# The last part of an entry moved between the first two product groups of the chunk or down half behind it

## The chip, the cores and the metric

The kernel runs on one core of a Trainium2 chip. The core has several engines that run side by side, each with an instruction queue of its own: TensorE (PE; its weight loads are listed as PEld) does the matrix products, VectorE (DVE) and ScalarE (ACT) do elementwise work, GpSimd (POOL) does little here, and SyncE (SP) issues the loads. The metric is the device time of one execution in microseconds (us), as the median of several runs.

## The reference

The model is a decoder trunk of two layers on 512 tokens of width 1024. Each layer has a mixer between two half-step SwiGLU feed-forward networks (FFNs), so there are four FFNs, and they are what the change touches.

```python
def swiglu(h, w_gate, w_up, w_down):
    return (jax.nn.silu(h @ w_gate) * (h @ w_up)) @ w_down

for i in range(DEPTH):                 # DEPTH = 2, D_MODEL = 1024, D_FF = 2816
    x = x + 0.5 * swiglu(rmsnorm(x, ffn1_norm[i]), ...)
    x = x + mixer(rmsnorm(x, mix_norm[i]))       # gated linear attention, then stick-breaking
    x = x + 0.5 * swiglu(rmsnorm(x, ffn2_norm[i]), ...)
return rmsnorm(x, final_norm)
```

All of it is float32. The weights come from HBM once each.

## The kernel before

**Precision by three products.** A float32 operand is split into a high part `h` and the rest `l`. ScalarE writes `h` (a cast, L138) and VectorE subtracts it from the operand to get `l` (L139). A product is then three matmuls, high by high, low by high and high by low, into one PSUM bank.

**Seven products for eight.** Most gate and up projections are done in chunks of 256 columns by a scheme of Strassen's kind (`seven`, from L682): the chunk's weights and the normed input are cut into halves, and seven products of sums of these halves do the work of eight. The sums of the weights (`sums_12`, `sums_34`: L694, L695, L700, L701) are made by VectorE, and their high and low parts are split like any operand. A product here is one call of `prod` (the matmul is L709): four steps of three matmuls, twelve in all. A chunk is two entries. Body 1 makes the products w (with the first block of the weights), then q, then more into w, and then z; body 2 goes on with w, q and w. The accumulators live on: after the first product ScalarE copies w into a second bank, z (L736), and both are accumulated further. The fourth product goes into z and the third into w, and the next products read-modify-write those banks. In between, ScalarE or VectorE takes out what has become final: `gate` is the silu of a gate chunk (L719, ScalarE) or the multiplication by the gate in an up chunk (L722, VectorE), L755 is a VectorE sum that the second activation of a gate chunk waits for, and L806 and L807 split the hidden activations again.

**The down projection** has two forms. A plain entry (`down`) makes a few output blocks `ps_d`, each followed by an addition to the residual x on VectorE (L339). For two groups of the hidden columns a down half (`seven_down`) uses the seven-product scheme: its products are L384, its copies of w into z L402, and each of its results is added to x by VectorE (L390). Its body 1 makes w, q, t2 (into w) and z; body 2 makes t3 (into w), b22 (into q) and t4 (into w), with a copy of w into u3 (L429) behind t3.

**The queue of entries.** All the weight matrices are cut into entries, in one list `feed.q`. An entry's `body` is a generator that yields after each group of products. `Feed.start` takes the next entry. First it splits the weights of this entry and of up to two behind it, as far as four large units go; it also forms the sums of the entries ahead and issues the loads of up to six entries. Then it returns the body. `Feed.entries` (L183) runs entries one by one: start, then each group to its end. With `ordered` it puts each group's matmuls behind the last matmul issued so far (`tc.issue_after(st["pe"])`), so that TensorE keeps the order of the program. Beyond such ties a scheduler places the instructions of each engine, and each engine runs its own in order.

In each FFN the order from the third chunk on is, with G and U for a gate and an up chunk, d for a plain down entry and sd for a down half: d d G2 U2 G3 d U3 d G4 U4 sd G5 U5 G6 sd d U6 d G7 d U7 d G8 U8 sd G9 U9 sd d G10 U10, and then the plain entries at the end. The text calls the two halves behind U4 and G6 the first pair, and those behind U8 and U9 the second pair.

**Buffers.** The raw weights of a chunk lie in `raw` (two buffers), the split ones in `wh` and `wl` (four each), the sums in `s` (four), the chunk's outputs in tiles with the tag `t` (five); PSUM has eight banks that are given out in a fixed turn.

Of the kernel before, what the change touches and what calls it, by code (L numbers as in the profile page):

```python
# [10 lines left out]
F32 = mybir.dt.float32  # L11
# [7 lines left out]
P = 128  # L19
T = 512  # L20
# [26 lines left out]
def decoder(ctx: ExitStack, tc: tile.TileContext, a: dict, out: bass.AP):  # L47
# [43 lines left out]
    class Chunk:  # L91
        def __init__(self, src, n, m):
            self.src, self.n, self.m, self.t = src, n, m, None
            self.pool = None
            self.few = False
# [12 lines left out]
    class Entry:  # L108
# [3 lines left out]

        def __init__(self, units, body):
            self.units, self.body, self.W, self.views = units, body, None, None

        def view(self):

# [24 lines left out]
    class Feed:  # L142
        def __init__(self):
            self.q, self.pos, self.cur = [], 0, None

        def start(self):
            i = self.pos
# [35 lines left out]
        def entries(self, n, ordered=False):  # L183

            self.finish()
            for _ in range(n):
                body, more = self.start(), True
                while more:
                    with tc.issue_after(st["pe"]) if ordered else ExitStack():
                        more = next(body, self) is not self  # L190

    feed = Feed()

# [118 lines left out]
    def down(w, r0, nf, hs, part, nxt, late=0):  # L312


        nd = KD // nf
        src = w[r0 : r0 + nf * P, part * nd * P : (part + 1) * nd * P]
        ch = Chunk(src.rearrange("(f p) c -> p f c", p=P), nf, nd * P)
        ch.few = True

        def body(W):  # L320
            (wh, wl), = W
            acc = []

            def prod(m, fs):
                if m == len(acc):
                    acc.append(psum("ps_d"))
                s = slice(m * P, (m + 1) * P)
                for f in fs:
                    mm3(acc[m], wh[:, f, s], wl[:, f, s], hs[f][0], hs[f][1], f == 0, f == nf - 1)

            if late:
                for m in range(nd):
                    prod(m, range(nf - late))
            for m in range(nd):
                prod(m, range(nf - late if late else 0, nf))
                ps = acc[m]
                k = part * nd + m
                x = pair(xs[k])
                nc.vector.scalar_tensor_tensor(  # L339
                    out=x, in0=flat(ps), scalar=0.5, in1=x, op0=ALU.mult, op1=ALU.add  # L340
                )
                if nxt is not None:
                    nxt(k)
                yield

        feed.q.append(Entry([(ch, lambda t: t, nf, nd * P)], body))

    def seven_down(pool, w, r0, hs, part):

        H = T // 2
        lower, upper = (
            Chunk(w[r0 : r0 + 4 * P, c : c + 256].rearrange("(f p) c -> p f c", p=P), 4, 256)
            for c in (part * 256, 512 + part * 256)
        )
        lower.few = upper.few = True
        v = {}

        def halves():  # L360

            lo, up = (c.load().rearrange("p (c two) d -> p two c d", two=2) for c in (lower, upper))
            return lo[:, 0], lo[:, 1], up[:, 0], up[:, 1]

        def sums_12(_):
            a11, _, a21, a22 = halves()
            s = v["s12"] = pool().tile([P, 4, 256], F32, tag="s", bufs=4, name="s12")
            nc.vector.tensor_tensor(out=s[:, 0:2], in0=a21, in1=a22, op=ALU.add)
            nc.vector.tensor_tensor(out=s[:, 2:4], in0=s[:, 0:2], in1=a11, op=ALU.subtract)
            return s  # L370

        def sums_34(_):
            a11, a12, a21, _ = halves()
            s = pool().tile([P, 4, 256], F32, tag="s", bufs=4, name="s34")
            nc.vector.tensor_tensor(out=s[:, 0:2], in0=a11, in1=a21, op=ALU.subtract)
            nc.vector.tensor_tensor(out=s[:, 2:4], in0=a12, in1=v["s12"][:, 2:4], op=ALU.subtract)
            return s

        def prod(ps, w, k0, m, b, first):
            for c in range(2):  # L380
                bh, bl = (turns(t) for t in hs[c][b])
                wh, wl = (t[:, k0 + c, m * P : (m + 1) * P] for t in w)
                for n, (l_, r_) in enumerate(((wh, bh), (wl, bh), (wh, bl))):
                    st["pe"] = nc.tensor.matmul(  # L384
                        ps, l_, r_, start=first and c + n == 0, stop=c == 1 and n == 2, skip_group_check=True
                    ).ins

        def add(m, up, col, ps):
            x = pair(xs[part * 2 + m + 4 * up][:, col * H : col * H + H])
            nc.vector.scalar_tensor_tensor(out=x, in0=ps, scalar=0.5, in1=x, op0=ALU.mult, op1=ALU.add)  # L390

        def body_1(W):
            a11, s, v["a2"] = W
            ws, zs, qs = [], [], []
            for m in range(2):
                ws.append(psum("ps_w")[:, 0:H])
                prod(ws[m], a11, 0, m, "b11", True)
            for m in range(2):


                zs.append(psum("ps_z")[:, 0:H])
                nc.scalar.copy(zs[m], ws[m])  # L402
            yield

            ps = psum("ps_q")
            for m in range(2):
                qs.append(ps[:, m * H : (m + 1) * H])
                prod(qs[m], s, 0, m, "t1", m == 0)
            for m in range(2):
                add(m, 1, 1, flat(qs[m]))  # L410
            yield
            for m in range(2):
                prod(ws[m], s, 2, m, "t2", False)
                add(m, 0, 1, flat(ws[m]))
            yield
            for m in range(2):
                prod(zs[m], v["a2"], 0, m, "b21", False)
                add(m, 0, 0, flat(zs[m]))
            v["w"], v["q"] = ws, qs
            yield  # L420

        def body_2(W):
            (s,) = W
            ws, qs = v["w"], v["q"]

            u3 = pool().tile([P, 2, H], F32, tag="c", bufs=1, name="u3")
            for m in range(2):
                prod(ws[m], s, 0, m, "t3", False)
                nc.scalar.copy(pair(u3[:, m]), flat(ws[m]))  # L429
                add(m, 1, 1, pair(u3[:, m]))  # L430
            yield
            for m in range(2):
                prod(qs[m], s, 2, m, "b22", False)
            for m in range(2):
                add(m, 0, 1, flat(qs[m]))
            yield
            for m in range(2):
                prod(ws[m], v["a2"], 2, m, "t4", False)
                add(m, 1, 0, flat(ws[m]))
            yield  # L440

        units = [(lower, lambda t: halves()[0], 2, 256), (lower, sums_12, 4, 256), (lower, lambda t: halves()[1::2], 4, 256)]
        feed.q.append(Entry(units, body_1))
        feed.q.append(Entry([(lower, sums_34, 4, 256)], body_2))

    def back_tok(w, r0, nf, hs, done):
# [30 lines left out]
    st = {}  # L477
# [129 lines left out]
    class FFN:  # L607
# [76 lines left out]
        def seven(self, ch, group=None):  # L684
# [5 lines left out]
            s12, v = [None], {}  # L690
# [35 lines left out]
            def body_1(W):  # L726


                a11, s, a2 = W
                v["a2"] = a2  # L730
                v["w"], v["q"] = psum("ps_w"), psum("ps_q")
                z = psum("ps_z")[:, 0:H]
                w, q = (v[n][:, 0:H] for n in "wq")
                o0, o1 = v["o"] = [self.tp.tile([P, T], F32, tag="t", name=n) for n in ("o0", "o1")]
                prod(w, a11, 0, half(0, 0))
                nc.scalar.copy(z, w)  # L736
                yield
                prod(q, s, 0, lambda j: self.t_half(0, j))
                nc.scalar.copy(pair(o1[:, H:T]), flat(q))
                yield  # L740
                prod(w, s, 4, lambda j: self.t_half(1, j), first=False)
                nc.scalar.copy(pair(o0[:, H:T]), flat(w))
                yield
                prod(z, a2, 0, half(4, 0), first=False)
                gate(o0, 0, flat(z))
                yield

            def body_2(W):
                (s,) = W
                w, q = (v[n][:, 0:H] for n in "wq")  # L750
                o0, o1 = v["o"]
# [9 lines left out]
                if group is not None:  # L761
                    close_0(o0)
                gate(o1, H, pair(o1[:, H:T]))
                yield
                prod(w, v["a2"], 0, lambda j: self.t_half(3, j), first=False, c0=P)
                gate(o1, 0, flat(w))
                if group is not None:
# [18 lines left out]

            units = [(ch, lambda t: t[:, 0:4, 0:P], 4, P), (ch, sums_12, KD, P), (ch, lambda t: t[:, 4:8], 4, 256)]
            feed.q.append(Entry(units, body_1))
            feed.q.append(Entry([(ch, sums_34, KD, P)], body_2))

        def t_half(self, i, j):
# [1114 lines left out]
```

## Time and profile before

| | |
|---|---|
| median of three runs | 1781.2 us (1780.84 to 1781.41) |
| the profiled execution | 1780.26 us |
| its span in the profile | 1778.3 us |
| granted clock of TensorE | 1.000 |
| moved by DMA | 179.24 MB, mean 101 GB/s |

The span is the time from the first to the last instruction that the profile shows; the execution's own time is 2 us longer, for what lies around it. The median of the runs without a profile is 0.9 us above the profiled execution. In the rows, the first number of a timeline is the start in us from the beginning of the span, the second the duration; then come engine, line, operation, output and inputs by the program's names without buffer numbers, and in brackets how long the engine had been idle before, and which instruction ended that. Matmuls are pipelined: a new one starts before the last one has ended, so one reads their starts, not their durations.

### The profile page before, as it was taken

What the parts mean: (1) busy time and instruction counts of PE and PEld (TensorE: products, weight loads), DVE (VectorE), ACT (ScalarE), POOL (GpSimd) and SP (SyncE); (2) the same over time, 40 slices, a digit from 0 to 9 for tenths busy, and PEclk for the clock granted to TensorE, in tenths of its full rate; (3) what the DMA queues carried; (4) which work ended last, traced back from release to release, by engine and by line L of the source; (5) the groups of instructions that cost most, each with busy time, mean ns of one, the idle gap of its engine ahead of it and who ended that gap; (6) DMA issues with size and microseconds to landing.
All of it is one profiled execution on the core that took longest, in us unless ns stands there. A gap on an engine that the chain in (4) does not pass through costs nothing.

```text
span 1778.3 us, 31182 instructions
## 1 busy us (share of the span) xinstructions
PE 1760.1 (99%) x12714; PEld 1631.7 (92%) x12714; DVE 1538.5 (87%) x2527; ACT 1050.5 (59%) x1830; POOL 9.8 (1%) x24
## 2 busy tenths in 40 slices
PE   9999999999999999999999999999999999999998
PEld 8999999889888899999889999999888888999997
DVE  8999798786878999889798988977898679998986
ACT  7556455554655556555555555655888755565554
POOL 0000000100000000000000000000000000000000
PEclk9999999999999999999999999999999999999999
DMA  5433334322122333333333333322212233333331
GB/s 167 142 115 112 107 96 132 93 71 72 49 95 95 104 110 119 107 107 108 109 93 119 96 119 103 124 84 83 83 48 72 71 95 119 110 105 111 105 126 52
DMA packets 178755, 179.24 MB, mean 101 GB/s; under 512 B 4082, under 2 KB 170276, under 8 KB 178612
## 3 DMA queue, kind: packets, MB, share of 16 engines
q1 hardware_dynamic: 177760, 175.91, 31.6%
q8 instruction: 99, 1.62, 0.4%
q0 software_dynamic: 608, 1.05, 0.2%
q14 instruction: 44, 0.36, 0.1%
q10 hardware_dynamic: 244, 0.29, 0.0%
HBM read 175.17 MB, written 2.10 MB: 100 GB/s over the span
## 4 chain that ended last, share of the span: by engine, by line
PE 64%; DVE 25%; ACT 7%; issue 3%; DMA 1%; SPq 0%; DVEq 0%; ACTq 0%
PE ps_w L709 14%; PE ps_d L80 12%; PE ps_f L80 8%; DVE wl L139 7%; PE ps_q L709 7%; PE ps_t L80 5%; PE ps_z L709 3%; PE ps_b L80 3%; ACT wh L138 3%; PE ps_w L384 2%; DVE x L390 2%; DVE ts L816 1%; PE ps_q L384 1%; PE ps_z L1394 1%; DVE xn L800 1%
## 5 line engine op out<-in xcount | busy, mean ns | idle before, releaser
L139 DVE TENSOR_TENSOR wl<-raw,wh 128x1024 fp32r<-128x1024 f32 x241 | 254.9, 1058 | 58.1 <-ACT wh L138 57.5
L138 ACT CAST wh<-raw 128x1024 fp32r<-128x1024 f32 x241 | 221.6, 920 | 72.4 <-PE ps_f L80 21.5
L139 DVE TENSOR_TENSOR wl<-s,wh 128x1024 fp32r<-128x1024 f32 x176 | 214.2, 1217 | 42.2 <-ACT wh L138 41.9
L138 ACT CAST wh<-s 128x1024 fp32r<-128x1024 f32 x176 | 184.2, 1047 | 102.9 <-DVE s L701 25.7
L709 PE MATMUL ps_w<-th,wh 128*128 128x256 f32 x864 | 239.8, 278 | 3.7 <-ACT ps_z L736 2.7
L709 PE MATMUL ps_w<-th,wl 128*128 128x256 f32 x864 | 237.6, 275 | 0.0
L709 PE MATMUL ps_w<-tl,wh 128*128 128x256 f32 x864 | 237.6, 275 | 0.0
L709 PEld LDWEIGHTS ps_w<-th,wh 128*128 128x128 f32 x864 | 165.8, 192 | 7.4 <-ACT ps_z L736 7.1
L80 PE MATMUL ps_f<-xh,wh 128*128 128x512 f32 x432 | 166.8, 387 | 0.9 <-DVE x L260 0.9
L709 PEld LDWEIGHTS ps_w<-tl,wh 128*128 128x128 f32 x864 | 165.9, 192 | 0.0
L709 PEld LDWEIGHTS ps_w<-th,wl 128*128 128x128 f32 x864 | 165.8, 192 | 0.0
L80 PE MATMUL ps_f<-xh,wl 128*128 128x512 f32 x432 | 164.2, 380 | 0.5 <-DVE wl L139 0.5
L80 PE MATMUL ps_f<-xl,wh 128*128 128x512 f32 x432 | 164.0, 380 | 0.0
L80 PE MATMUL ps_d<-hl,wh 128*128 128x512 f32 x416 | 158.0, 380 | 0.9 <-DVE hl L807 0.8
L80 PE MATMUL ps_d<-hh,wh 128*128 128x512 f32 x416 | 157.7, 379 | 0.2 <-ACT hh L806 0.2
L80 PE MATMUL ps_d<-hh,wl 128*128 128x512 f32 x416 | 157.7, 379 | 0.0
L138 ACT CAST wh<-rawd 128x1024 fp32r<-128x1024 f32 (+1 forms) x100 | 82.9, 845 | 60.1 <-PE ps_d L80 45.2
L139 DVE TENSOR_TENSOR wl<-rawd,wh 128x1024 fp32r<-128x1024 f32 (+1 forms) x100 | 95.7, 961 | 14.7 <-ACT wh L138 14.7
L80 PEld LDWEIGHTS ps_f<-xh,wh 128*128 128x128 f32 x432 | 81.7, 189 | 12.1 <-DVE x L260 1.3
L80 PEld LDWEIGHTS ps_f<-xl,wh 128*128 128x128 f32 x432 | 81.7, 189 | 11.5
L80 PEld LDWEIGHTS ps_f<-xh,wl 128*128 128x128 f32 x432 | 81.7, 189 | 11.1 <-DVE wl L139 0.9
L339 DVE SCALAR_TENSOR_TENSOR x<-ps_d,x 128x512 f32<-128x512 f32 x120 | 79.8, 682 | 13.8 <-PE ps_d L80 13.7
(352 smaller groups left out, 5247.9 us busy)
## 6 DMA issues: line engine op xcount, KB each, us to landing
raw<-in_ffn_w_gate_dram SPq DMA_DIRECT2D x43, 1024.0 KB, 5.4
raw<-in_ffn_w_up_dram SPq DMA_DIRECT2D x43, 1024.0 KB, 5.3
rawd<-in_ffn_w_down_dram SPq DMA_DIRECT2D x84, 512.0 KB, 3.6
raw<-in_gla_w_in_dram SPq DMA_DIRECT2D x12, 1024.0 KB, 5.3
raw<-in_sb_w_in_dram SPq DMA_DIRECT2D x16, 512.0 KB, 3.7
raw<-in_gla_w_out_dram SPq DMA_DIRECT2D x4, 1024.0 KB, 5.2
raw<-in_sb_w_in_dram SPq DMA_DIRECT2D x4, 1024.0 KB, 5.0
raw<-in_sb_w_out_dram SPq DMA_DIRECT2D x4, 1024.0 KB, 5.1
```

Of the source, the lines that this page charges most:

```text
L80: st["pe"] = nc.tensor.matmul(ps, l, r, start=first, stop=last).ins
L138: st["cut"] = nc.scalar.copy(h[:, k], part).ins
L139: nc.vector.tensor_tensor(out=l[:, k], in0=part, in1=h[:, k].bitcast(F32), op=ALU.subtract)
L339: nc.vector.scalar_tensor_tensor(out=x, in0=flat(ps), scalar=0.5, in1=x, op0=ALU.mult, op1=ALU.add)
L384: st["pe"] = nc.tensor.matmul(ps, l_, r_, start=first and c + n == 0, stop=c == 1 and n == 2, skip_group_check=True).ins
L390: nc.vector.scalar_tensor_tensor(out=x, in0=ps, scalar=0.5, in1=x, op0=ALU.mult, op1=ALU.add)
L709: st["pe"] = nc.tensor.matmul(o, l_, r_, start=first and j + n == 0, stop=j == 3 and n == 2, skip_group_check=True).ins
L800: nc.vector.scalar_tensor_tensor(out=t, in0=xs[k], scalar=g, in1=st["R"], op0=ALU.mult, op1=ALU.mult)
L816: nc.vector.tensor_tensor(out=o, in0=p, in1=q, op=ALU.subtract)
L1394: nc.tensor.matmul(o_, l_, r_, start=first, stop=last, skip_group_check=True)
```

## The change

An entry can be marked as one that leads (`lead`): body 1 of every seven-product chunk and of every seven-product down half is. Three kinds of bodies now say "tail" at their last group: a plain down entry ahead of its last output block, body 2 of a chunk ahead of its last product, and body 2 of a down half ahead of its t4 products. When `Feed.entries` meets "tail" and the next entry leads, it leaves the old body there, starts the next entry (with the splits, sums and loads that this brings), issues its first group, then the rest of the old body behind it, and then the second group of the new one. The tiles `o0` and `o1` of a chunk are taken after the first group instead of before, so that the buffers `t` go round in the same order as before. No instruction is added or taken away.

```diff
@@ -112,6 +112,7 @@
 
         def __init__(self, units, body):
             self.units, self.body, self.W, self.views = units, body, None, None
+            self.lead = False
 
         def view(self):
 
@@ -142,6 +143,7 @@
     class Feed:
         def __init__(self):
             self.q, self.pos, self.cur = [], 0, None
+            self.tail = None
 
         def start(self):
             i = self.pos
@@ -184,10 +186,18 @@
 
             self.finish()
             for _ in range(n):
-                body, more = self.start(), True
-                while more:
+                body, got = self.start(), None
+                while got is not self:
                     with tc.issue_after(st["pe"]) if ordered else ExitStack():
-                        more = next(body, self) is not self
+                        got = next(body, self)
+                    if self.tail is not None:
+                        tail, self.tail = self.tail, None
+                        with tc.issue_after(st["pe"]):
+                            for _ in tail:
+                                pass
+                    if got == "tail" and self.pos < len(self.q) and self.q[self.pos].lead:
+                        self.tail = body
+                        break
 
     feed = Feed()
 
@@ -341,7 +351,7 @@
                 )
                 if nxt is not None:
                     nxt(k)
-                yield
+                yield "tail" if m == nd - 2 else None
 
         feed.q.append(Entry([(ch, lambda t: t, nf, nd * P)], body))
 
@@ -433,7 +443,7 @@
                 prod(qs[m], s, 2, m, "b22", False)
             for m in range(2):
                 add(m, 0, 1, flat(qs[m]))
-            yield
+            yield "tail"
             for m in range(2):
                 prod(ws[m], v["a2"], 2, m, "t4", False)
                 add(m, 1, 0, flat(ws[m]))
@@ -441,6 +451,7 @@
 
         units = [(lower, lambda t: halves()[0], 2, 256), (lower, sums_12, 4, 256), (lower, lambda t: halves()[1::2], 4, 256)]
         feed.q.append(Entry(units, body_1))
+        feed.q[-1].lead = True
         feed.q.append(Entry([(lower, sums_34, 4, 256)], body_2))
 
     def back_tok(w, r0, nf, hs, done):
@@ -731,10 +742,10 @@
                 v["w"], v["q"] = psum("ps_w"), psum("ps_q")
                 z = psum("ps_z")[:, 0:H]
                 w, q = (v[n][:, 0:H] for n in "wq")
-                o0, o1 = v["o"] = [self.tp.tile([P, T], F32, tag="t", name=n) for n in ("o0", "o1")]
                 prod(w, a11, 0, half(0, 0))
                 nc.scalar.copy(z, w)
                 yield
+                o0, o1 = v["o"] = [self.tp.tile([P, T], F32, tag="t", name=n) for n in ("o0", "o1")]
                 prod(q, s, 0, lambda j: self.t_half(0, j))
                 nc.scalar.copy(pair(o1[:, H:T]), flat(q))
                 yield
@@ -761,7 +772,7 @@
                 if group is not None:
                     close_0(o0)
                 gate(o1, H, pair(o1[:, H:T]))
-                yield
+                yield "tail"
                 prod(w, v["a2"], 0, lambda j: self.t_half(3, j), first=False, c0=P)
                 gate(o1, 0, flat(w))
                 if group is not None:
@@ -786,6 +797,7 @@
 
             units = [(ch, lambda t: t[:, 0:4, 0:P], 4, P), (ch, sums_12, KD, P), (ch, lambda t: t[:, 4:8], 4, 256)]
             feed.q.append(Entry(units, body_1))
+            feed.q[-1].lead = True
             feed.q.append(Entry([(ch, sums_34, KD, P)], body_2))
 
         def t_half(self, i, j):
```

## The prediction

> **What bounds the kernel now.** I read the page's busy line and chain first, then the list of waits, then what the two product helpers wait for, and last the timelines around the stalls.
>
> ```profile
> span 1778.3 us, 31182 instructions
> PE 1760.1 (99%) x12714; PEld 1631.7 (92%) x12714; DVE 1538.5 (87%) x2527; ACT 1050.5 (59%) x1830; POOL 9.8 (1%) x24
> PE 64%; DVE 25%; ACT 7%; issue 3%; DMA 1%; SPq 0%; DVEq 0%; ACTq 0%
> ```
>
> TensorE is busy 99% of the span, so what an edit of order alone can give is its idle time, 18.2 us. VectorE is busy 87%, and a quarter of the chain that ended last runs over it: it is the second bound, and that decides this case.
>
> The waits that the edit concerns are those of a product on the copy z<-w (L736), which ScalarE makes right behind the first group. In these rows the columns are total us, times, longest; the second and third come from what line 709 and line 384 wait for.
>
> ```profile
> PEld ps_w L709 <- ACT ps_z L736: 7.1, 18, 1.4
> ...
>   ACT ps_z L736: 9.8, 27
> ...
>   DVE x L390: 1.3, 6
> ```
>
> There are 18 places, 7.1 us by the weight loads (9.8 over both kinds of record, which overlap). One of them, in the up chunk ahead of the first down half:
>
> ```profile
> 124.71 0.28 PE L709 MATMUL ps_q<-th,wl 128*128 128x256 f32 x1
> 124.82 0.28 PE L709 MATMUL ps_q<-tl,wh 128*128 128x256 f32 x1
> 125.26 0.38 PE L709 MATMUL ps_w<-th,wh 128*128 128x256 f32 x1 [0.16 <-ACT ps_z L736]
> 125.47 0.28 PE L709 MATMUL ps_w<-th,wl 128*128 128x256 f32 x1
> ...
> 122.03 0.42 ACT L719 ACTIVATE o<-o 128x256 f32<-128x256 f32 x1 [1.83 <-DVE o L755]
> 122.36 1.03 ACT L138 CAST wh<-s 128x1024 fp32r<-128x1024 f32 x1
> 123.29 0.42 ACT L719 ACTIVATE o<-o 128x256 f32<-128x256 f32 x1
> 123.61 0.36 ACT L719 ACTIVATE o<-ps_w 128x256 f32<-128x256 f32 x1
> 123.88 1.07 ACT L138 CAST wh<-s 128x1024 fp32r<-128x1024 f32 x1
> 124.81 0.40 ACT L736 COPY ps_z<-ps_w 128x256 f32<-128x256 f32 x1
> ```
>
> Matmuls start 0.11 apart (124.71 to 124.82), so a product of twelve takes 1.34. Here 0.44 passes before the next one and 0.21 after it: 0.33 of waiting and 0.10 of restart. ScalarE is late because the activation at 122.03 waits for a VectorE sum (L755), and VectorE is late because it has no pause in this stretch. The columns here are the window, its length, and busy time (with instructions) of TensorE, its weight loads, VectorE, ScalarE, GpSimd; clock; DMA share; GB/s:
>
> ```profile
> 106.00:135.00 29.00, 28.84 (x236) 28.00 (x235) 28.86 (x50) 17.22 (x31) 0.00 (x0) 1.00 0.35 109
> 222.00:251.00 29.00, 28.79 (x235) 27.96 (x235) 28.86 (x49) 17.62 (x32) 0.00 (x0) 1.00 0.35 110
> ```
>
> VectorE has 0.14 of 29 us left in both. So the kernel has two regimes: where VectorE has slack, TensorE's stall is a matter of order; where it has none, the stall is how TensorE waits for VectorE, whichever wait shows it.
>
> **The change, part by part.** The number of instructions is the same on every engine, and the orders on SP and GpSimd are the same too, so no queue of theirs is passed by a DMA. What moves is order on TensorE, ScalarE and VectorE.
>
> *First product early, old part between.* Each of the four FFNs has 22 chunks and down halves that are marked to lead, 88 in all, and each follows an entry with a last part. The copy z<-w then has 2.68 us instead of 1.34 before the product that needs it. It also stands ahead of the old part's activation and gate work on ScalarE. At the place shown it would follow the activation at 123.29 and end near 124.0, so the direct wait goes. Over 18 places I take 7.1 + 18 x 0.10 = 8.9 us as what goes at these places. Whether it stays gone depends on the regime.
>
> *Places with slack on VectorE.* They are the second chunk or the one before it in each FFN. These rows are what waited for line 736 in the windows 60:105, 600:650, 925:975 and 1490:1535:
>
> ```profile
>   PEld ps_w L709: 0.4, 1
>   PEld ps_w L709: 0.2, 1
>   PEld ps_w L709: 1.4, 1
>   PEld ps_w L709: 0.5, 1
> ```
>
> That is 2.5, with restarts 2.9. The 1.4 isn't wholly won: on ScalarE that copy stands behind an activation that waits 2.94 for VectorE.
>
> ```profile
> 946.38 0.42 ACT L719 ACTIVATE o<-o 128x256 f32<-128x256 f32 x1 [2.94 <-DVE o L755]
> ...
> 947.64 0.41 ACT L719 ACTIVATE o<-o 128x256 f32<-128x256 f32 x1
> ...
> 949.15 0.37 ACT L736 COPY ps_z<-ps_w 128x256 f32<-128x256 f32 x1
> ...
> 949.58 0.19 PEld L709 LDWEIGHTS ps_w<-th,wh 128*128 128x128 f32 x1 [1.38 <-ACT ps_z L736]
> ```
>
> Behind the activation at 947.64 (0.33 from start to start, as 123.29 to 123.61) it would run from 947.97 to 948.34; the load could start at 949.58 - 1.38 = 948.20 and starts some 0.06 behind the copy's end, as now. About 0.2 stays, and with its restart 0.3. Kept: 2.6 us.
>
> *Places inside VectorE's unbroken stretches.* The other 14. The product t3 of a down half goes on in the ps_w that a VectorE add (L390) reads, and it waits for that add even now:
>
> ```profile
> 137.31 0.28 PE L384 MATMUL ps_z<-hl,wh 128*128 128x256 f32 x1
> 137.53 0.38 PE L384 MATMUL ps_w<-nh,wh 128*128 128x256 f32 x1
> ...
> 175.42 0.28 PE L384 MATMUL ps_z<-hl,wh 128*128 128x256 f32 x1
> 175.53 0.32 PE L384 MATMUL ps_w<-nh,wh 128*128 128x256 f32 x1
> ...
> 281.69 0.28 PE L384 MATMUL ps_z<-hl,wh 128*128 128x256 f32 x1
> 281.95 0.38 PE L384 MATMUL ps_w<-nh,wh 128*128 128x256 f32 x1
> ```
>
> The gaps are 0.22, 0.11 and 0.26. An add at the end of unbroken VectorE work doesn't come sooner because TensorE does, so a gain of 0.3 upstream returns as 0.3 more wait at t3. Net zero, if VectorE's work ahead of the add stays the same. It doesn't.
>
> *VectorE work that moves ahead of that add.* The new entry is started earlier, and starting issues the sums and subtractions of entries to come. I counted, from the order of both programs, what stands before each add; prices are start to start. In the first halves of both pairs (eight places) two 512-wide operations of 0.60 come in and a 1024-wide one of 1.13 goes out: +0.07, which I take at nothing, bounds 0 and 8 x 0.07 = 0.6. In the second half of the first pair the sum at 175.67 comes ahead of the adds:
>
> ```profile
> 173.74 0.68 DVE L139 TENSOR_TENSOR wl<-raw,wh 128x512 fp32r<-128x512 f32 x1
> 174.34 0.75 DVE L390 SCALAR_TENSOR_TENSOR x<-ps_q,x 128x256 f32<-128x256 f32 x2
> 175.01 0.74 DVE L390 SCALAR_TENSOR_TENSOR x<-ps_w,x 128x256 f32<-128x256 f32 x2
> 175.67 0.68 DVE L701 TENSOR_TENSOR s<-raw,s 128x512 f32<-128x512 f32 x1
> ```
>
> From 175.67 to the next it takes 0.60 (as 173.74 to 174.34), so t3 comes 0.60 later: the first of the two adds at 175.01 ends about 175.43, and t3 starts at 175.53 now, with nothing to spare. In the second half of the second pair the subtraction at 282.14 and one more 512-wide difference come ahead, 1.20, less the pause of 0.38, in which some of it fits:
>
> ```profile
> 280.21 0.69 DVE L807 TENSOR_TENSOR hl<-o,hh 128x512 fp32r<-128x512 f32 x1 [0.38 <-ACT hh L806]
> ...
> 281.48 0.75 DVE L390 SCALAR_TENSOR_TENSOR x<-ps_w,x 128x256 f32<-128x256 f32 x2
> 282.14 0.68 DVE L139 TENSOR_TENSOR wl<-raw,wh 128x512 fp32r<-128x512 f32 x1
> ```
>
> That is 0.82. The order is the same in all four FFNs, so the loss is 4 x (0.60 + 0.82) = 5.7 us. From below it could be a gain, if VectorE came out of its stretches earlier because its own waits for ScalarE's casts shrink; it ends at 1.3, all that t3 waits now. From above it is 4 x (0.60 + 1.20) + 0.6 = 7.8.
>
> *The waits that are added.* The old part is tied to the product before it on TensorE; its own operands have been there since its entry began. On ScalarE the copy waits for the first group, and behind it stand the old part's activation and the next cast. They wait for a product that comes 1.34 later than now, so nothing comes sooner or later by more than one product. The last part's two adds or gate (0.34 each) come as much later, with a PSUM bank held longer; I take that at nothing, because the banks turn over eight buffers, and at most one step of 0.42 in a place from above.
>
> *Loads.* The first product needs its split operand 1.34 earlier; the next sums need their 1 MB load, 5.3 us from issue to landing, earlier too. VectorE might wait there, ahead of its stretch, where it pauses anyway; zero, and up to 0.4 for each FFN.
>
> **The sum.** -2.6 + 5.7 = +3.1 us. The profiled execution took 1780.3 and the median of three runs is 1781.2, 0.9 above it; so 1783.4 beside the profiled one, 1784.3 for a median.
>
> **The rule that speaks against this.** VectorE's 28.86 of 29 us is the row. The Trainium skill, Perfetto Trace Analysis, section Optimization Strategy, says to look for the gaps of the engine that limits, find what they wait for, and have that start sooner or finish faster; taken for TensorE's 18 gaps that is this edit, and the sum by it would be 1781.2 - 8.9 = 1772.3, the first rival below. The same section says that the most-contended engine can differ between regimes of a kernel. By that sentence the gaps within 106 to 135 are VectorE's, and the sum stays as above.
>
> **The rivals.**
> (A) *The stalls simply go.* All 18 places win and no other wait grows: 1781.2 - 8.9 = 1772.3. For it: VectorE waits 114 us for casts of ScalarE over the span, and reordering ScalarE could shorten some of it. Against it: in the stretches shown VectorE has 0.14 of 29 us to give.
>
> ```profile
> DVE wl L139 <- ACT wh L138: 114.0, 91, 6.5
> ```
>
> (B) *VectorE's moved work is hidden.* The sums that come early fall in pauses that open up, t3 is no later than now, and the slack places pay: 1781.2 - 2.6 = 1778.6, or up to 1781 where some of the loss remains. The existing wait at t3 of only 1.3 us over six places speaks for it; the absence of pauses against.
>
> (C) *Slower still: t3 pays for all of it and the slack places give nothing.* If the early sums wait for their load, the pause of VectorE before the stretch is used up, the stretch begins no sooner, and the 2.6 returns at the first t3. Then 1781.2 + 7.8 = 1789.0. It decides if the load lands more than a pause later than VectorE gets to it.
>
> **How the numbers follow.** My forecast, 1784.3, with its own range 1781 to 1786.5, has 0.50; A 0.13; B 0.17; C, 1786.5 and up, 0.20. The range 1778.6 to 1789.0 takes in the ends of B and C and leaves out A and a little beyond C. A measurement of this kernel can tell about 0.2% from no change, 3.6 us, so the bounds are 1777.6 and 1784.8. Faster is A, 0.13. Same is B and six tenths of the forecast, 0.47. Slower is C and the rest, 0.40.
>
> **What the profile after would show.** The waits on the z copy drop from 18 places to four or fewer, under 1 us. The waits of line 384's products on the VectorE add, now 1.3 us, rise to some 10 us; t3's gap in the second half of the first pair goes from 0.11 to about 1. VectorE stays full in 106 to 135. The wait of 1.38 at 949.58 becomes about 0.2. I am wrong if the t3 waits stay near 1.3 us, or if the time goes to a third place, above all to a cast that is late for a first product or to a PSUM bank.

## The result and the profile after

The changed kernel takes 1788.95 us as the median of six runs (1787.93 to 1792.96), the kernel before beside it 1781.06 (1780.36 to 1781.55). The ratio is 1.0046 with a 95% interval of 1.0036 to 1.0057: slower, by 7.9 us where 3.1 was forecast. The profiled execution took 1789.4 us, 9.1 more than that of before.

The page of the changed kernel, its span, busy line and chain by engine:

```profile
span 1787.5 us, 31209 instructions
PE 1757.4 (98%) x12714; PEld 1630.4 (91%) x12714; DVE 1541.5 (86%) x2527; ACT 1051.7 (59%) x1830; POOL 9.8 (1%) x24
PE 63%; DVE 27%; ACT 5%; issue 3%; DMA 2%; DVEq 0%; SPq 0%; ACTq 0%
```

Each engine does the same number of instructions as before; the total of 31209 against 31182 differs by semaphore instructions alone. The line numbers have moved by some ten: the products of a chunk are L720 (before L709), the z copy L746 (L736), the copy into o0 L753 (L742), a down half's products L394 (L384), its adds L400 (L390), the split's subtraction L140 (L139). The waits of TensorE's weight loads and one of VectorE, then what waited for the z copy (from the view of line 746):

```profile
PEld ps_w L394 <- DVE x L400: 15.4, 16, 1.8
PEld ps_w L720 <- ACT o L753: 3.9, 5, 1.7
...
DVE s L705 <- DMA raw<-in_ffn_w_up_dram: 3.1, 3, 1.3
...
  PEld ps_w L720: 0.2, 1
```

The wait that the edit aims at is gone: one place of 0.2 us is left of 18 places and 7.1 us. In its place t3 waits 15.4 us at all 16 down halves (before 1.3 at 6), and a wait that was hardly there before, on the copy into o0, has come with 3.9 us.

Where along an FFN the time goes is seen from starts of the same product in both traces: the shift (after less before) at one product less the shift at the product where the stage begins. The stages run from the second product of the first seven-product chunk, G2, to that of G3, from there to that of U3, and then from one t3 to the next.

| stage | FFN 1 | FFN 2 | FFN 3 | FFN 4 | sum, us | forecast |
|---|---|---|---|---|---|---|
| first chunks, G2 to G3 | -0.50 | -0.26 | -1.21 | -0.53 | -2.5 | -2.6 |
| G3 to U3 | 0.71 | 0.89 | 1.78 | 0.53 | 3.9 | 0 |
| to t3, first half of first pair | 0.12 | 0.06 | 0.13 | 0.10 | 0.4 | 0 |
| to t3, second half of first pair | 0.50 | 0.70 | 1.57 | 0.59 | 3.4 | 2.4 |
| to t3, first half of second pair | 0.11 | 0.09 | 0.12 | 0.18 | 0.5 | 0 |
| to t3, second half of second pair | 0.73 | 0.78 | 0.85 | 0.88 | 3.2 | 3.3 |

The sum is 8.9; the two profiled executions differ by 9.1, and the other 0.2 lie between FFN 1 and FFN 2. So the gain of the first chunks is there as forecast, and t3's loss is where the forecast put it, 7.5 in the last four rows against 5.7. What the forecast doesn't have is the 3.9 us between G3 and U3.

### The profile page after: what moved, and what is told of

Read it like the earlier page. It is cut to its first block, busy times and chain, and to the rows that moved or that the text cites. A ratio compares the mean times of both kernels' runs of the same rounds, so it can differ in the third digit from the quotient of the medians.

```text
span 1787.5 us, 31209 instructions
## 1 busy us (share of the span) xinstructions
PE 1757.4 (98%) x12714; PEld 1630.4 (91%) x12714; DVE 1541.5 (86%) x2527; ACT 1051.7 (59%) x1830; POOL 9.8 (1%) x24
## 4 chain that ended last, share of the span: by engine, by line
PE 63%; DVE 27%; ACT 5%; issue 3%; DMA 2%; DVEq 0%; SPq 0%; ACTq 0%
PE ps_w L720 15%; PE ps_d L80 12%; DVE wl L140 8%; PE ps_f L80 8%; PE ps_q L720 7%; PE ps_t L80 5%; PE ps_z L720 4%; PE ps_b L80 3%; PE ps_w L394 2%; DVE x L400 2%; ACT wh L139 2%; DMA raw<-in_ffn_w_up_dram 1%; DVE ts L828 1%; PE ps_z L1406 1%; DVE nl L819 1%
## 5 line engine op out<-in xcount | busy, mean ns | idle before, releaser
L140 DVE TENSOR_TENSOR wl<-raw,wh 128x1024 fp32r<-128x1024 f32 x241 | 255.0, 1058 | 65.4 <-ACT wh L139 63.6
L139 ACT CAST wh<-raw 128x1024 fp32r<-128x1024 f32 x241 | 221.5, 920 | 72.3 <-PE ps_f L80 21.5
L140 DVE TENSOR_TENSOR wl<-s,wh 128x1024 fp32r<-128x1024 f32 x176 | 214.2, 1217 | 35.5 <-ACT wh L139 35.5
L720 PE MATMUL ps_w<-th,wh 128*128 128x256 f32 x864 | 238.3, 276 | 2.9 <-ACT o L753 2.8
L139 ACT CAST wh<-s 128x1024 fp32r<-128x1024 f32 x176 | 184.0, 1046 | 91.2 <-DVE s L706 39.2
L720 PE MATMUL ps_w<-th,wl 128*128 128x256 f32 x864 | 237.6, 275 | 0.0
L720 PE MATMUL ps_w<-tl,wh 128*128 128x256 f32 x864 | 237.6, 275 | 0.0
L720 PEld LDWEIGHTS ps_w<-th,wh 128*128 128x128 f32 x864 | 165.8, 192 | 4.1 <-ACT o L753 3.9
L720 PEld LDWEIGHTS ps_w<-tl,wh 128*128 128x128 f32 x864 | 165.9, 192 | 0.0
L720 PEld LDWEIGHTS ps_w<-th,wl 128*128 128x128 f32 x864 | 165.9, 192 | 0.0
L140 DVE TENSOR_TENSOR wl<-rawd,wh 128x1024 fp32r<-128x1024 f32 (+1 forms) x100 | 95.7, 961 | 17.3 <-ACT wh L139 17.3
L139 ACT CAST wh<-rawd 128x1024 fp32r<-128x1024 f32 (+1 forms) x100 | 82.8, 844 | 44.5 <-PE ps_d L80 20.2
L80 PEld LDWEIGHTS ps_f<-xh,wh 128*128 128x128 f32 x432 | 81.7, 189 | 12.3 <-DVE x L270 1.5
L80 PEld LDWEIGHTS ps_f<-xh,wl 128*128 128x128 f32 x432 | 81.7, 189 | 11.2 <-DVE wl L140 0.9
```

The costliest lines, as they stand in the source:

```text
L80: st["pe"] = nc.tensor.matmul(ps, l, r, start=first, stop=last).ins
L139: st["cut"] = nc.scalar.copy(h[:, k], part).ins
L140: nc.vector.tensor_tensor(out=l[:, k], in0=part, in1=h[:, k].bitcast(F32), op=ALU.subtract)
L720: st["pe"] = nc.tensor.matmul(o, l_, r_, start=first and j + n == 0, stop=j == 3 and n == 2, skip_group_check=True).ins
```

## The experiments

**e1_later: the look-ahead behind the old part.** Was the moved VectorE work moved because the new entry is started early?

```diff
-        def start(self):
+        def start(self, ahead=True):       # ahead(): the splits, sums and loads that start() issued
...
-                body, got = self.start(), None
+                body, got = self.start(self.tail is None), None
...
                             for _ in tail:
                                 pass
+                        self.ahead()
```

> The changed kernel, but where an old part comes between, the look-ahead of the new entry (splits, sums and loads of the entries behind it) is issued behind the old part instead of ahead of the first group; the order on TensorE stays that of the changed kernel. Theory 1 (the early look-ahead puts VectorE work in front of the adds that t3 waits for, and puts a late load in front of VectorE): the losses between the fourth chunk and the last down half, about 7.5 us, go, the first places win 2.6 again, and the wait of the fifth chunk's third product on the copy into o0, which I put down to the displaced old part, stays with about 0.7 in each FFN: 1781.1 - 2.6 + 2.8 = 1781.3. Theory 2 (the early look-ahead makes that wait too): it goes as well, 1778.5. Theory 3 (t3 is late because the old part's own activations, casts and adds come later, not because of the look-ahead): the waits at t3 stay at about 15 us, and the time at 1787 to 1789.

Measured: 1787.7 us, ratio 1.0036 (1.0024 to 1.0049). The waits of the weight loads of this kernel, whose products are L727 and L401:

```profile
PEld ps_w L401 <- DVE x L407: 15.0, 16, 1.5
PEld ps_w L727 <- ACT u L772: 2.0, 4, 0.6
PEld ps_w L727 <- ACT o L760: 0.3, 1, 0.3
```

Theory 1 fell: t3 waits as long as before this edit, and the time is theory 3's. VectorE has the same work of later entries in front of the adds as in the changed kernel, here a split and a sum in the second half of the second pair:

```profile
279.08 0.69 DVE L140 TENSOR_TENSOR wl<-raw,wh 128x512 fp32r<-128x512 f32 x1
...
280.03 0.68 DVE L718 TENSOR_TENSOR s<-raw 128x512 f32<-128x512 f32 x1
...
283.50 0.38 PE L401 MATMUL ps_w<-nh,wh 128*128 128x256 f32 x1 [1.11 <-DVE x L407]
```

By the program, the start of the down half's body 2 issues these two. Neither the change nor this edit moves that start: the change brings forward the start of a body 1, and this edit puts the look-ahead of that start back. So the early start isn't what puts them ahead of the adds. e8_nosd_nog3, beside e2_nog3, shows that the displaced part in the down halves does; why the scheduler then places them so isn't shown.

The first stage did change. From G3 to U3 this kernel loses 2.3 us instead of 3.9. No VectorE sum waits for U3's load any more, and the wait on the copy into o0 is down to one place of 0.3, but TensorE now waits 2.0 on the copy into u3 (L772). For the copy into o0, then, theory 2 has it.

**e2_nog3: one lead less.** G3 follows the up chunk U2, whose last part closes half of a hidden block: a gate on VectorE, a cast on ScalarE, four sums on VectorE, their casts on ScalarE.

```diff
                             self.seven(g)
+                            if c == 3:
+                                feed.q[-2].lead = False
```

> The changed kernel, but the gate chunk behind the first up chunk of the second group doesn't lead, so the last part of that up chunk, which closes the group's first hidden block, stays where it was. Theory 1 (at this one place the displaced last part holds up ScalarE, four places of 0.4 to 1.7 us and 0.1 of restart each): the waits on the copy into o0 go, the early places keep their 2.6 us, the t3 waits stay: 1788.95 - 4.1 = 1784.9. Theory 2 (VectorE is the bound there too and takes the gain back at the first t3): the gain returns as longer t3 waits in the first down half, and the time stays within 1 us of 1788.95.

Measured: 1784.7 us, ratio 1.0021 (1.0012 to 1.0030). Its waits of TensorE's matmuls hold one row of a seven-product line, t3's:

```profile
PE ps_w L394 <- DVE x L400: 12.0, 16, 1.6
```

The waits on the copy into o0 are gone but for one of 0.3 us, nothing is lost between G3 and U3 any more (0.01 by the starts), and 4.2 us come back, as theory 1 has it. How the waits arose is seen in FFN 1. The changed kernel's VectorE (two sums of U3's weights, the gate, two splits, the last of the four sums), its ScalarE and the product; then the kernel before; then e1_later:

```profile
78.87 0.69 DVE L705 TENSOR_TENSOR s<-raw 128x512 f32<-128x512 f32 x1
79.59 0.69 DVE L706 TENSOR_TENSOR s<-s,raw 128x512 f32<-128x512 f32 x1
...
85.97 0.41 DVE L733 TENSOR_TENSOR o<-ps_w,o 128x256 f32<-128x256 f32 x1
86.30 0.68 DVE L140 TENSOR_TENSOR wl<-raw,wh 128x512 fp32r<-128x512 f32 x1
86.90 1.21 DVE L140 TENSOR_TENSOR wl<-rawd,wh 128x1024 fp32r<-128x1024 f32 x1
88.03 0.41 DVE L889 TENSOR_TENSOR ts<-o,ts 128x256 f32<-128x256 f32 x1
...
86.41 0.63 ACT L818 CAST hh<-o 128x512 fp32r<-128x512 f32 x1 [0.58 <-DVE o L733]
...
88.48 0.41 ACT L818 CAST nh<-ts 128x256 fp32r<-128x256 f32 x1 [0.35 <-DVE ts L889]
88.79 0.37 ACT L753 COPY o<-ps_w 128x256 f32<-128x256 f32 x1
...
89.21 0.38 PE L720 MATMUL ps_w<-th,wh 128*128 128x256 f32 x1 [0.45 <-ACT o L753]
```

```profile
85.13 0.42 DVE L722 TENSOR_TENSOR o<-ps_w,o 128x256 f32<-128x256 f32 x1
...
88.07 0.37 ACT L742 COPY o<-ps_w 128x256 f32<-128x256 f32 x1
...
89.11 0.28 PE L709 MATMUL ps_w<-th,wh 128*128 128x256 f32 x1
```

```profile
85.31 0.42 DVE L740 TENSOR_TENSOR o<-ps_w,o 128x256 f32<-128x256 f32 x1
...
87.69 0.37 ACT L760 COPY o<-ps_w 128x256 f32<-128x256 f32 x1
```

On ScalarE the last part's casts stand ahead of G3's copies in all three kernels. Before, the copy into o0 ended at 88.44, 0.67 ahead of the product that needs it. In the changed kernel the last part's own product comes 0.82 later (its first matmul at 83.24 instead of 82.42) and the gate 0.84 later. But the later product doesn't make the stall by itself: in e1_later it comes at 83.26, and there the gate is only 0.18 later than before, and the copy into o0 ends at 88.06, in time for the product at 88.62. The changed kernel differs from e1_later in VectorE's order. Two sums of U3's weights stand far ahead of the gate (78.87 to 80.20), and two splits, 1.73 together, stand between the gate and the last of the four sums, for which the cast at 88.48 waits 0.35. So the copy into o0 ends at 89.16, where TensorE could have begun at 88.60, 1.34 behind the product before.

The loss thus takes both: a chain of gate, sums and casts that has less time because its part is displaced, and other entries' work that VectorE does in between. With that work later, in e1_later, it is the copy into u3 that is late: on ScalarE it stands behind a cast that waits 1.16 for a sum of U3's weights. What the first chunks win at the z copy, 2.5 us, is lost at G3, and more.

**e3_later_nog3: both edits.** The diffs of e1_later and e2_nog3 together.

> Both edits, the late look-ahead and no displaced part at the gate chunk behind the first up chunk of the second group. Theory 1 (two separate losses): only the gain of the early places is left, 1781.1 - 2.6 = 1778.5, with t3 waits of about 7 us in which the other fourteen gains return. Theory 2 (without the two losses all the gains stay): 1781.1 - 8.9 = 1772.2. Theory 3 (t3 is late for another reason): 1784 to 1785.

Measured: 1784.66 us, ratio 1.0019 (1.0011 to 1.0028), the same as e2_nog3 alone. t3 waits 15.0 us at 16 places. Once G3 doesn't lead, the place of this look-ahead in the program is worth nothing.

**e4_early_later: only the first two chunks lead.** The look-ahead is that of e1_later.

```diff
-            feed.q[-1].lead = True             # in seven()
+            feed.q[-1].lead = lead             # True for the gate and the up chunk with c == 2
...
-        feed.q[-1].lead = True                 # in seven_down()
```

> Only the first two seven-product chunks of each FFN lead, with the late look-ahead; all other places are as in the kernel before. If the gains inside VectorE's unbroken stretches really return at t3, this is worth as much as the run with both edits at all other places: 1778.5, waits on the z copy left at 14 places, about 4.6 us. If those gains are kept, it is up to 6 us slower than that run.

Measured: 1778.63 us, ratio 0.9988 (0.9979 to 0.9997). This is the forecast's term of -2.6, measured by itself as -2.5 (by the interval -0.5 to -3.7; by the starts -2.5 from G2 to G3, as in the changed kernel). The z copy's waits left are those of the 14 other places and 0.2 of the 1.4:

```profile
PEld ps_w L726 <- ACT ps_z L752: 4.9, 15, 0.4
PEld ps_w L401 <- DVE x L407: 1.5, 7, 0.3
```

**e5_hold: VectorE's look-ahead behind the adds.** The start of body 2 of a down half ties the splits and sums of later entries behind the adds that t3 waits for (a split's cast on ScalarE is tied with it); the old parts stay displaced.

```diff
+            with tc.issue_after(st["add"]) if self.q[i].hold else ExitStack():
                 (splits and sums of the entries ahead)
...
                 prod(ws[m], s, 2, m, "t2", False)
-                add(m, 0, 1, flat(ws[m]))
+                st["add"] = add(m, 0, 1, flat(ws[m]))
...
         feed.q.append(Entry([(lower, sums_34, 4, 256)], body_2))
+        feed.q[-1].hold = True
```

> The changed kernel, but in the second body of a down half the look-ahead's VectorE work (splits and sums of later entries) is tied behind the two adds of ps_w that t3 waits for; the displaced parts and the order on TensorE stay. By the order of the programs this takes 1.2 us of VectorE work from in front of these adds in three of the four down halves of an FFN and 1.8 in the other, against t3 waits of 0.65, 0.88, 0.66 and 1.27. Theory 1 (t3 is late because of other entries' work that VectorE does first, and VectorE's total is not the limit): the t3 waits fall from 15 us to about 1, nothing takes their place, 1788.95 - 15.5 = 1773.5. Theory 2 (VectorE has no time left in its stretches, so work that is put off is late somewhere else): t3 waits fall, but waits on splits, on the copy into o0 or on the z copy rise by nearly as much, and the time stays above 1784. Theory 3 (t3 waits for the displaced part's own chain): t3 waits stay.

Measured: 1773.15 us, ratio 0.9953 (0.9939 to 0.9966), 7.9 us faster than the kernel before and 15.8 faster than the changed one. Waits of the weight loads, one of VectorE, and the window of the forecast, first of the changed kernel, then of this one:

```profile
PEld ps_w L722 <- ACT o L755: 4.8, 5, 2.2
PEld ps_w L395 <- DVE x L401: 0.7, 4, 0.2
...
DVE s L707 <- DMA raw<-in_ffn_w_up_dram: 4.1, 3, 2.2
...
106.00:135.00 29.00, 29.00 (x240) 28.36 (x239) 28.82 (x49) 17.18 (x32) 0.00 (x0) 1.00 0.35 109
...
106.00:135.00 29.00, 29.00 (x240) 28.37 (x239) 27.85 (x48) 18.23 (x34) 0.00 (x0) 1.00 0.33 110
```

Theory 1 holds to 0.4 us: t3's waits went from 15.4 to 0.7. What grew is the loss between G3 and U3, 6.5 us by the starts instead of 3.9, with longer waits for U3's load; but that is in the profiled execution, at 1776.4 the longest of the five. Theory 2, that VectorE has no time left, falls: VectorE has 1.15 of 29 us left in the window, where the changed kernel leaves it 0.18. TensorE has no gap in this window in either kernel; in the changed one it waits behind it, at t3.

**e6_nog3_hold: the tie, and G3 doesn't lead.** The diffs of e5_hold and e2_nog3 together.

> The tie of the run before, and the gate chunk behind the first up chunk of the second group doesn't lead. Theory 1: both losses go, 1784.7 - 15.5 = 1769.2, that is all the gains at the z copy are kept (1781.1 - 8.9 = 1772.2) and t3's old 1.6 us with restarts go too. Theory 2: above 1780.

Measured: 1769.84 us, ratio 0.9936 (0.9924 to 0.9949). Both losses go, as theory 1 has it.

**e7_before_hold: the tie alone, on the kernel before.** The diff of e5_hold, applied to the kernel before.

> The kernel before with the tie alone, nothing displaced. Theory 1: its t3 waits (10 places, 1.6 us, and 1.0 of restarts) go and the 18 waits on the z copy stay: 1781.1 - 2.6 = 1778.5. If the tie alone brings as much as the tie with the displaced parts, the z copy's waits too come from VectorE's order: then 1770 to 1773. Theory 2: 1781, the waits only change place.

Measured: 1777.17 us, ratio 0.9978 (0.9969 to 0.9988). The tie takes t3's waits away; the z copy still makes TensorE wait, at 14 places for as long as at 18:

```profile
PEld ps_w L712 <- ACT ps_z L739: 7.1, 14, 1.4
```

In the window 106 to 135 VectorE is busy 27.57 of 29 us in this kernel, and TensorE has the gap of the kernel before (28.85 busy). So there the z copy's wait doesn't need a full VectorE. The two edits are worth 3.9 us (this one) and 7.3 (from here to e6_nog3_hold), and the displaced parts bring that only where t3 can make use of it.

**e8_nosd_nog3: VectorE's order as before, all z places displaced.** The down halves and G3 don't lead, there is no tie; the diff of e2_nog3, and

```diff
         feed.q.append(Entry(units, body_1))
-        feed.q[-1].lead = True
         feed.q.append(Entry([(lower, sums_34, 4, 256)], body_2))
```

> The changed kernel, but neither the down halves nor the gate chunk behind the first up chunk of the second group lead. VectorE's order in front of the four adds of an FFN that t3 waits for is then, operation for operation, that of the kernel before, while all 18 places of the z copy have an old part between. This is the forecast's step 'net zero, if VectorE's work ahead of the add stays the same' by itself. Theory 1 (as forecast: within the stretches the gains return at t3): 1781.1 - 2.6 = 1778.5, t3 waits of about 6 to 7 us. Theory 2 (the gains are kept, VectorE's fullness was no limit): 1781.1 - 8.9 = 1772.2, t3 waits near the 1.6 of before.

Measured: 1779.55 us, ratio 0.9992 (0.9983 to 1.0001). Theory 1 is the nearer by far:

```profile
PEld ps_w L394 <- DVE x L400: 4.4, 16, 0.3
PEld ps_w L394 <- ACT ps_z L412: 3.7, 13, 0.8
...
106.00:135.00 29.00, 29.00 (x237) 28.17 (x237) 28.86 (x48) 17.76 (x32) 0.00 (x0) 1.00 0.34 110
```

With VectorE's order ahead of the adds unchanged, the gains return: t3's waits rise from 1.3 to 4.4 us, and 3.7 come at the down half's own copies of w. So the forecast's sentence that a gain upstream returns at t3 is true for a given order of VectorE. Its reason, that VectorE has no time left, isn't: VectorE is as full here, 28.86 of 29 us, as in the kernel before, but e5_hold shows that it needn't be.

**e9_nog3_hold1: the tie in the second half of each pair only.** As e6_nog3_hold, with

```diff
-        feed.q[-1].hold = True
+        feed.q[-1].hold = part == 1
```

> As the run with the tie and without the one lead, but the tie only in the second half of each pair. If each half's t3 wait is made by the work in front of its own add, the waits of the second halves (0.9 and 1.3 in each FFN, 1.8 once) go and those of the first halves (0.6 to 0.7) stay: 1784.7 - 9.5 - 0.8 of restarts = 1774.4. If work that is put off at one half comes back at the next, the first halves' waits grow, and the time is above 1776.

Measured: 1775.75 us, ratio 0.9969 (0.9956 to 0.9981), 1.4 above the expectation and just under the 1776 of the other reading, so the trace has to decide.

```profile
PEld ps_w L395 <- DVE x L401: 6.0, 12, 0.7
```

The starts of the matmuls show 0.61 and 0.66 of waiting in the first halves, as without the tie, and 0.14 or none in the second. So the first halves' waits didn't grow: work that is put off at one half doesn't come back at the next. Of the 1.4, some 1.0 is what is left in four second halves, 0.14 and a restart of 0.10 each (an estimate from the starts).

**e10_nosd_nog3_hold: the tie, and neither the down halves nor G3 lead.** The diffs of e8_nosd_nog3 (with that of e2_nog3) and of e5_hold together.

> As the run with the tie and without the one lead, but the down halves don't lead either. If the displaced part in front of a down half brings nothing once VectorE's order is tied, the time is that of the run with them, 1769.8 within 1 us. If it brings something, the waits of the down half's own products on the copies of w grow, and it is slower by up to 2 us.

Measured: 1768.87 us (1768.71 to 1770.51), ratio 0.9932 (0.9919 to 0.9944): 12.3 us faster than the kernel before and 20.1 faster than the changed one, the fastest of all, though not clearly faster than e6_nog3_hold. So, with the tie, the displaced part in front of a down half brings nothing. Its page and its waits:

```profile
span 1766.8 us, 31159 instructions
PE 84%; DVE 11%; ACT 3%; issue 1%; DMA 1%; SPq 0%; DVEq 0%; ACTq 0%
...
PEld ps_w L723 <- ACT o L756: 0.3, 1, 0.3
PEld ps_w L723 <- ACT ps_z L749: 0.2, 1, 0.2
```

Those two are the only waits left on a product into ps_w; the chain that ended last runs over VectorE for 11% of the span where it was 25% before. The adds of the second half of the second pair, with the split that stands ahead of them in the changed kernel:

```profile
277.65 0.75 DVE L401 SCALAR_TENSOR_TENSOR x<-ps_q,x 128x256 f32<-128x256 f32 x2
278.32 0.75 DVE L401 SCALAR_TENSOR_TENSOR x<-ps_w,x 128x256 f32<-128x256 f32 x2
278.98 0.68 DVE L140 TENSOR_TENSOR wl<-raw,wh 128x512 fp32r<-128x512 f32 x1
...
279.15 0.28 PE L395 MATMUL ps_z<-hl,wh 128*128 128x256 f32 x1
279.26 0.28 PE L395 MATMUL ps_w<-nh,wh 128*128 128x256 f32 x1
```

The first add on ps_w ends near 278.74, half a microsecond ahead of t3, which starts 0.11 behind the matmul before it.

## Why the prediction was wrong, point by point

**The direct wait goes: right.** "The copy z<-w then has 2.68 us instead of 1.34 before the product that needs it", and the waits fell to 0.2 us in one place.

**Second halves, +5.7: right.** The table has 3.4 + 3.2 = 6.6. The order of VectorE in the changed kernel, in the second half of the second pair, shows the two operations that the forecast counted ahead of the adds, and the pause of 0.38 gone:

```profile
279.20 0.69 DVE L140 TENSOR_TENSOR wl<-raw,wh 128x512 fp32r<-128x512 f32 x1
279.81 0.42 DVE L733 TENSOR_TENSOR o<-ps_w,o 128x256 f32<-128x256 f32 x1
280.14 0.68 DVE L711 TENSOR_TENSOR s<-raw 128x512 f32<-128x512 f32 x1
280.74 1.22 DVE L140 TENSOR_TENSOR wl<-rawd,wh 128x1024 fp32r<-128x1024 f32 x1
281.88 0.68 DVE L819 TENSOR_TENSOR hl<-o,hh 128x512 fp32r<-128x512 f32 x1
282.48 0.74 DVE L400 SCALAR_TENSOR_TENSOR x<-ps_q,x 128x256 f32<-128x256 f32 x2
283.14 0.74 DVE L400 SCALAR_TENSOR_TENSOR x<-ps_w,x 128x256 f32<-128x256 f32 x2
...
283.61 0.38 PE L394 MATMUL ps_w<-nh,wh 128*128 128x256 f32 x1 [1.10 <-DVE x L400]
```

The first pair has 3.4 where 2.4 was forecast, and 1.0 of that is FFN 3, where VectorE stands idle for 1.00 ahead of a sum (L705) that waits for a gate load. The other three lose 0.50 to 0.70 here; in e1_later that sum waits 0.52, and this half loses 1.11 instead of 1.57. So the two go together, though no run changes the load alone. The reason that the forecast gave, that the new entry's early start issues this work early, is wrong: the start of body 2 issues it, which the change leaves where it was, and it stands in the same place in e1_later.

**First halves, 0 of at most 0.6: too low by 0.9 over eight places,** 0.11 each. Why it is more than the 0.07 of the count is open.

**Places with slack, -2.6: right.** The changed kernel is 2.5 us ahead at G3, and e4_early_later has 2.5 by itself.

**The waits that are added, 0: this is the step that failed.** The sentence says that the last part's adds or gate come as much later, and "I take that at nothing". For ScalarE the forecast says that nothing comes later by more than one product, 1.34 us, but it doesn't ask how much the copies behind have to spare. At G3 the displaced part closes half a hidden block, and the copy into o0 behind its casts had 0.67 us to spare in FFN 1. The term measured 3.9 us, 0.53 to 1.78 in each FFN where the forecast's bound was 0.42 in a place. With that one lead gone it is 0.0 by the starts, and 4.2 us come back by the medians (e2_nog3).

The term of the loads, "zero, and up to 0.4 for each FFN", had its part. In three FFNs VectorE waited for the load of U3's weights, 3.1 us in all. With the look-ahead issued later (e1_later) these waits are gone and 2.3 of the 3.9 remain, so the early sums with their loads are worth up to 1.6. The loads alone don't make the stall: FFN 1 loses 0.71 without a wait for a load, and FFN 4 loses least, 0.53, with one of 1.09. How the loss divides in each FFN is open.

**The sum.** 3.9 between G3 and U3, 0.1 in the first chunks, 0.9 in the first halves and 0.9 in the second make the 5.8 us between 3.1 and 8.9. One of the forecast's own signs of being wrong came true: the time went to a third place.

**The regimes: the reading was wrong, though its terms were nearly right.** The forecast says of the stretches without slack that "the stall is how TensorE waits for VectorE". But the 99.5% of VectorE in 106 to 135 holds work of later entries, some of which can wait. e5_hold puts it off, and both the t3 waits and the z waits are gone but for 0.9 us. VectorE's order was the limit, not the amount of its work. The Trainium skill, Perfetto Trace Analysis, section Identifying the Most-Contended Engine, calls the occupancy of VectorE a fair measure of how near it is to its roofline. Read as a sign of what limits TensorE, it doesn't hold in this stretch: VectorE's 99.5% over 29 us stood in a kernel that became 12.3 us faster by order alone (e10_nosd_nog3_hold).

**The rivals.** A, 1772.3, is near what the displaced parts bring once the adds' order is mended and G3 doesn't lead (1769.8, in which t3's old waits are gone too). C named the right time, 1789.0, and late loads as its condition. Half of its mechanism came: t3 pays 7.5 where C has 7.8, and the 2.5 won do return. But they return at G3's copy, ahead of the first t3, and there 3.9 are lost, with loads late in three of the four FFNs. That C's sum came out within 0.1 us is luck.

## What to carry to other kernels

When a part is displaced behind another, step through every engine on which the displaced part has instructions, and ask what of the new work stands behind them there, what else can be placed between them, and how much slack is left. An engine that is full over a stretch may be full of work that isn't due; look at what stands directly ahead of the instruction that the limiting engine waits for, and try to put that off before calling the engine a bound. And a gain upstream that "returns" at a later wait is a hint that this later wait is worth mending first: here the tie alone brought 3.9 us, the displaced parts with it 7.9, or 11.2 with G3 left out, and the displaced parts without it a loss of 7.9.

## What the runs showed that was not expected

Issuing the look-ahead of the leading entries later in the program changed t3's waits by 0.4 us of 15.4 (e1_later), while a tie of body 2's look-ahead took 14.7 of them (e5_hold). The full VectorE was no limit: with the same number of instructions in the whole program, its busy time in the window 106 to 135 fell from 28.86 us in the kernel before to 27.74 (e10_nosd_nog3_hold), and TensorE has no gap there, as in the changed kernel.

```profile
106.00:135.00 29.00, 29.00 (x239) 28.36 (x239) 27.74 (x47) 17.95 (x32) 0.00 (x0) 1.00 0.36 109
```
